# A charge for overlap and a margin against GpSimd in a kernel recorder's count

## The chip, the cores and the metric

The program runs on one core of one Trainium2 chip. The metric is the device time of one execution in microseconds (us). TensorE is PE in the profile (its weight loads are PEld), VectorE is DVE, ScalarE is ACT, GpSimd is POOL and SyncE is SP.

## What is computed

The reference is one inference step of a two-layer decoder trunk in float32. A prompt of 16 learned meta tokens and 1024 tokens and a group of 8 samples of 4 tokens share the weights; the model width is 1024. Cut to what matters:

```python
for l in range(2):
    proj = x @ w_in[l]                      # 4 mixers of 256 columns each, with gates
    a = gated_delta_net(conv(proj.a))       # 4 heads, 64x64 state, chunks of 64
    b = hgrn2(proj.b); c = gla(proj.c)      # gated linear recurrences
    d = retention(rope(proj.d))             # fixed decay
    m = concat(norm(a), norm(b), norm(c), norm(d)) * silu(gates) @ w_out[l]
    x = layer_norm(ALPHA * x + m)
    x = layer_norm(ALPHA * x + (silu(x @ w_gate[l]) * (x @ w_up[l])) @ w_down[l])
```

It returns the outputs of both groups, the last rows of the convolution and the states of all heads.

## The kernel before

All tokens stand as 1072 columns in three groups of 304, 384 and 384 (`GROUPS`). A dense product is made of fp32r products: weights and activations are split into a high and a low part (`splits`, `split_out`, `ffn_split`), and each product is three matmuls on line 833. The high part is a copy on ACT (L855), the low part a subtraction, which may run on DVE (L864) or on POOL (L866). A layer has three stretches: the input projection with the four mixers working beside it, the output projection with a layer norm, and the feed-forward part (FFN) with its layer norm. The small products of the mixers fill the same PE queue as the dense ones.

The order of all instructions is found when the program is built, by a recorder (`Kern.run`). Each part of the work is a thread: `main` for the dense products, four mixer workers, the weight loads and splits, the layer norms, and small helpers. A thread gives operations (`Op`), each with an engine, a cost in nanoseconds and what it reads and writes. The recorder keeps a clock for each engine (`clk`) and the time at which each range of memory is ready (`t_data`). Over and over it takes, among the operations whose predecessors are recorded, the one with the earliest start, and `emit` records it, advances its engine's clock by the cost, and marks its output ready a latency later (`LATENCY`). Every engine then runs its own instructions in the recorded order, with semaphores between the engines. So the costs in this count never stand on the chip; they only decide the order, and the engine where there is a choice.

A choice is offered by `tt2`: a `tensor_tensor` with no operand in PSUM is given as a pair, one for DVE and one for POOL, and the recorder takes the one that ends first in its count. The costs before are `68 + 1.042 * n` for DVE and `147 + 2.1 * n` for POOL, with n the elements in a partition. Some operations have no choice. On POOL always: the zeroing memsets (`zero`, L927), two products in each `delta_unit`, and the gain and shift of the residual in `residual` (512 wide) and `save_x` (256 wide), in which `tt` is called with "POOL". On DVE always: all that reads PSUM (tile `banks`), and `stt` (L877), `ts` (L902, unless the pair offers ACT), `dcopy` (L907), scans, transposes and the statistics of the norms.

Of the kernel before, what the change touches and what calls it, by code (L numbers as in the profile page):

```python
# [213 lines left out]
class V:  # L214
# [4 lines left out]
    def __init__(self, ap, sp, lo, hi, part=0):  # L219
        self.ap, self.sp, self.lo, self.hi, self.part = ap, sp, lo, hi, part  # L220
# [54 lines left out]
class P(V):  # L275
# [41 lines left out]
    def range(self):  # L317
        return range(self.h.at + self.lo, self.h.at + self.hi)
# [14 lines left out]
    return tuple(range(row // 32, (row + a) // 32)), tuple(range(col // 32, (col + b) // 32)), (a, b)  # L333


LATENCY = {"PE": 196.0, "DVE": 128.0, "ACT": 131.0, "POOL": 76.0}


class Wait:
# [95 lines left out]
class Kern:  # L435
    def __init__(self, tc, ins, outs):
        self.tc, self.nc, self.i, self.o = tc, tc.nc, ins, outs
        self.clk = {e: 0.0 for e in ("PE", "ACT", "DVE", "POOL", "SP", "DMA", "HW")}
        self.mode, self.pe_end = (128, 128), 0.0
        self.t_load = [0.0] * 4  # L440
        self.t_start, self.t_end = {}, [[0.0] * 4 for _ in range(4)]
        self.switches = 0
        self.tick, self.cols, self.warm = 0, 0.0, False
        self.duty, self.duty_t = 0.0, 0.0
        self.nc.scalar.preload_act_table_set(TABLES[AF.Exp])
        self.w_t = np.zeros(NCOL // 16 + 2)
        self.r_t = np.zeros(NCOL // 16 + 2)
        self.pw_t = [0.0] * 8
        self.pr_t = [0.0] * 8
        self.dw_t = {}  # L450
        self.table = TABLES[AF.Exp]
        self.clk["ACT"] = 1283.0
        self.threads = []
        self.flags = {}
        self.cur = None
# [185 lines left out]
    def emit(self, op, t0):  # L641
        e = op.eng
        cost = op.cost
        if e == "ACT" and op.table and op.table != self.table:
            self.nc.scalar.preload_act_table_set(op.table)  # L645
            self.table = op.table
            t0 += 1283
        op.fn()
        if e == "SP":
            self.clk["SP"] = t0 + 60  # L650
            q = max(t0 + 600, self.clk["HW"])
            self.clk["HW"] = q + 480
            d0 = max(q + 900, self.clk["DMA"])
            self.clk["DMA"] = d0 + cost
            end = rend = d0 + cost + 500
        else:
            if e == "PE":
                rq, cq, mode = op.tile
                k = int(t0 / TICK)
                if k > self.tick:  # L660
                    self.warm = k == self.tick + 1 and self.cols >= FULL
                    self.tick, self.cols = k, 0.0
                self.cols += op.work
                slow = 1 if self.warm else 2
                td = self.t_data(op)
                if mode != self.mode:
                    td = max(td, self.pe_end + DRAIN)
                    self.mode = mode
                    self.switches += 1
                for _ in range(op.passes):  # L670
                    a = max(td, self.t_start.get((rq, cq), 0.0), *(self.t_load[r] for r in rq)) + WLOAD * op.cols * slow
                    b = max(a, *(self.t_end[r][c] for r in rq for c in cq))
                    f = b + op.cost * slow
                    for r in rq:
                        self.t_load[r] = a
                        for c in cq:
                            self.t_end[r][c] = f
                    self.t_start[rq, cq] = b
                t0 = max(t0, b) if len(rq) + len(cq) < 8 else t0
                cost = f - t0 if len(rq) + len(cq) == 8 else 6.0  # L680
                self.pe_end = max(self.pe_end, f)
                self.duty = self.duty * math.exp((self.duty_t - t0 - cost) / SPAN) + op.work / 2.4 / SPAN
                self.duty_t = t0 + cost
            self.clk[e] = t0 + cost
            end = rend = (f if e == "PE" else t0 + cost) + LATENCY[e]
        for v in op.rd:
            if v.sp == "s":
                a, b = v.lo // 16, (v.hi + 15) // 16
                np.maximum(self.r_t[a:b], rend, out=self.r_t[a:b])
            elif v.sp == "p":  # L690
                for k in v.range():
                    self.pr_t[k] = max(self.pr_t[k], rend)
        for v in op.wr:
            if v.sp == "s":
                a, b = v.lo // 16, (v.hi + 15) // 16
                np.maximum(self.w_t[a:b], end, out=self.w_t[a:b])
            elif v.sp == "p":
                for k in v.range():
                    self.pw_t[k] = max(self.pw_t[k], end)
            else:  # L700
                self.dw_t[v.lo] = max(self.dw_t.get(v.lo, 0.0), end)
# [47 lines left out]
    def run(self):  # L749
        self.cur = None  # L750
        while True:
# [9 lines left out]
            for th in self.threads:  # L761
                open_bank = False
                for pos, e in enumerate(th.q):
                    if not e.ops:
                        continue
                    new = any(h.at is None for h in e.banks)
                    skip = e.deps or new and open_bank
                    open_bank |= new
                    if skip:
                        continue  # L770
                    tb = 0.0
                    if new:
                        hs = [h for h in e.banks if h.at is None]
                        ks = self.places(hs)
                        if ks is None:
                            continue
                        tb = max(self.bank_time(k, h.n) for k, h in zip(ks, hs))
                    if e.td is None:
                        e.td = [max(self.t_data(o) for o in e.run)] if len(e.run) > 1 else [self.t_data(o) for o in e.ops]
                    pick = None  # L780
                    for op, td in zip(e.ops, e.td):
                        t = max(td, tb, self.clk[op.eng])
                        x = t
                        if op.eng == "ACT" and op.table and op.table != self.table:
                            x += 1283
                        if pick is None or x + op.cost < pick[0] + pick[1].cost:
                            pick = (x, op)
                    if pick[1].eng == "PE":
                        tiled = pick[1].tile[2] != FULLM
                        if tiled and self.mode == FULLM:  # L790
                            pick = (max(pick[0], max(e.td[0], tb) + HOLD), pick[1])
                        elif not tiled and self.mode != FULLM:
                            pick = (max(pick[0], self.clk["PE"] + SLACK), pick[1])
                    k = (pick[0], URGENT if pick[1].eng != "PE" and any(h.main for h in e.banks) else th.prio, pos)
                    if th.name == "main" and pick[1].eng == "PE" and self.duty < KEEP and pick[0] <= self.clk["PE"]:
                        k = (self.clk["PE"] - 1.0, th.prio, pos)
                    if best is None or k < best[0]:
                        best = (k, pick[1], th, e)
# [3 lines left out]
            _, op, th, e = best  # L802
# [58 lines left out]
    def tt(self, out, a, b, op, eng="DVE"):  # L861
        if eng == "DVE":
            return Op("DVE", 68 + 1.042 * out.n,
                      lambda: self.nc.vector.tensor_tensor(out=out.x(), in0=a.x(), in1=b.x(), op=op), (a, b), (out,))  # L864
        return Op("POOL", 147 + 2.1 * out.n,
                  lambda: self.nc.gpsimd.tensor_tensor(out=out.x(), in0=a.x(), in1=b.x(), op=op), (a, b), (out,), 27.0)  # L866

    def stt(self, out, a, s, b, op0, op1):
# [1784 lines left out]
```

## Time and profile before

| | us |
|---|---|
| median of 3 runs | 3169.23 (3167.81 to 3171.99) |
| profiled execution, its own time | 3172.53 |
| span of that execution | 3170.8 |
| PE busy | 3018.0 |
| DVE busy | 1731.3 |
| ACT busy | 1111.1 |
| POOL busy | 529.6 |

The span runs from the first to the last instruction; the execution's own time is 1.7 us longer. The mean granted clock of TensorE is 0.977 of full speed. The chain that ended last is the way back from the last instruction to whatever released it, step by step; here it reaches back to 554 us. Matmuls are pipelined and their ends are modelled, so that a busy PE can still be waiting for operands between matmuls.

### The profile page before, as it was taken

How to read it: one execution, taken by the hardware profiler on the slowest of the kernel's cores; microseconds unless marked ns; L12 is line 12 of the kernel's file. 1: busy time of each engine (PE TensorE's matmuls, PEld its weight loads, DVE VectorE, ACT ScalarE, POOL GpSimd, SP SyncE). 2: the span in 40 equal slices, each digit the busy share in tenths (PEclk: the TensorE clock that was granted, in tenths of full speed). 3: DMA queues.
4: the chain of work that ended last, by engine and by line, in shares of the span. 5: the costliest groups of instructions: out<-in, count | busy, mean ns of one | idle time of the engine just before them, and what ended most of it. 6: DMA issues, size and time to landing. Idle time of an engine off the chain costs nothing.

```text
span 3170.8 us, 65772 instructions
## 1 busy us (share of the span) xinstructions
PE 3018.0 (95%) x27758; PEld 2733.2 (86%) x27758; DVE 1731.3 (55%) x3978; ACT 1111.1 (35%) x2310; POOL 529.6 (17%) x617
## 2 busy tenths in 40 slices
PE   7999999989999999999999989999999999999996
PEld 5778887878899999999977778879789999999996
DVE  8886668556633333333497856783774333333336
ACT  5454577432411111111264437763433111111113
POOL 3412213010600000000044211230115000000001
PEclk8999999999999999999999999999999999999998
DMA  5310221241111111111033102123511111111112
GB/s 199 110 49 27 66 64 61 90 158 57 60 54 47 47 40 41 53 47 47 34 125 92 48 26 69 62 65 96 177 47 63 41 40 54 47 47 47 47 40 75
DMA packets 121030, 210.94 MB, mean 67 GB/s; under 512 B 32336, under 2 KB 81488, under 8 KB 120608
## 3 DMA queue, kind: packets, MB, share of 16 engines
q1 hardware_dynamic: 120736, 206.75, 19.7%
q8 instruction: 217, 3.56, 0.5%
q14 instruction: 77, 0.63, 0.1%
HBM read 162.28 MB, written 40.04 MB: 64 GB/s over the span
## 4 chain that ended last, share of the span: by engine, by line
PE 65%; DVE 9%; ACT 3%; DMA 2%; issue 2%; POOL 1%; SPq 0%; DVEq 0%; ACTq 0%; POOLq 0%
PE banks L833 63%; DVE H L864 2%; DVE R L864 2%; DVE H L877 1%; PE banks L839 1%; DVE P L864 1%; ACT H L858 1%; DVE H L902 1%; DVE H L1012 1%; ACT R L855 1%; ACT P L858 1%; ACT L645 0%; DMA H<-XR 0%; DMA H<-OF 0%; POOL H L866 0%
## 5 line engine op out<-in xcount | busy, mean ns | idle before, releaser
L833 PE MATMUL banks<-R 128*128 128x384 f32 (+3 forms) x11840 | 2106.8, 334 | 36.7 <-DVE R L864 13.8
L833 PEld LDWEIGHTS banks<-R 128*128 128x128 f32 x11840 | 1939.0, 191 | 103.9 <-DVE R L864 23.1
L864 DVE TENSOR_TENSOR H<-H,banks 128x512 f32<-128x512 f32 (+6 forms) x722 | 407.3, 568 | 534.6 <-PE banks L833 531.8
L864 DVE TENSOR_TENSOR R<-H,R 128x1024 fp32r<-128x1024 f32 (+5 forms) x356 | 347.8, 987 | 444.6 <-ACT R L855 442.2
L855 ACT CAST R<-H 128x1024 fp32r<-128x1024 f32 (+3 forms) x358 | 284.7, 811 | 803.8 <-PE banks L833 712.0
L833 PE MATMUL banks<-R,P 128*128 128x512 f32 x1584 | 371.7, 394 | 0.0
L833 PEld LDWEIGHTS banks<-R,P 128*128 128x128 f32 x1584 | 296.2, 188 | 66.8 <-issue 0.6
L866 POOL TENSOR_TENSOR H<-H 128x256 f32<-128x256 f32 (+10 forms) x267 | 237.3, 903 | 331.0 <-ACT H L858 81.8
L866 POOL TENSOR_TENSOR P<-H,P 128x384 fp32r<-128x384 f32 (+7 forms) x49 | 73.6, 1503 | 1303.6 <-ACT P L855 1283.4
L858 ACT ACTIVATE H<-H 128x384 f32<-128x384 f32 (+11 forms) x455 | 189.7, 434 | 191.0 <-DVE H L1014 78.9
L833 PE MATMUL banks<-H 32*32 32x32 f32 (+15 forms) x6134 | 203.7, 224 | 22.2 <-issue 8.3
L833 PEld LDWEIGHTS banks<-H 32*32 32x32 f32 (+9 forms) x6134 | 146.8, 121 | 79.5 <-issue 42.8
L833 PE MATMUL banks<-P 32*32 32x32 f32 (+10 forms) x5982 | 170.7, 215 | 26.5 <-DVE P L864 12.4
L833 PEld LDWEIGHTS banks<-P 32*32 32x32 f32 (+6 forms) x5982 | 124.2, 118 | 75.7 <-issue 36.9
L855 ACT COPY H<-banks 128x384 f32<-128x384 f32 (+14 forms) x305 | 112.0, 374 | 219.9 <-PE banks L833 176.6
L855 ACT CAST P<-H 128x304 fp32r<-128x304 f32 (+2 forms) x132 | 64.3, 487 | 284.8 <-DVE H L864 284.8
L864 DVE TENSOR_TENSOR H<-H 128x384 f32<-128x384 f32 (+12 forms) x310 | 131.8, 442 | 50.5 <-ACT H L858 28.9
L858 ACT ACTIVATE H<-banks 128x384 f32<-128x384 f32 (+5 forms) x169 | 72.0, 429 | 228.9 <-PE banks L833 223.5
L839 PE MATMUL banks<-H 128*128 128x128 f32 (+3 forms) x639 | 114.0, 302 | 36.1 <-DVE H L902 16.2
L833 PE MATMUL banks<-P,R 128*128 128x304 f32 (+1 forms) x1056 | 147.4, 299 | 0.0
L833 PEld LDWEIGHTS banks<-P,R 128*128 128x128 f32 x1056 | 145.9, 188 | 0.0
L839 PEld LDWEIGHTS banks<-H 128*128 128x128 f32 (+3 forms) x639 | 77.9, 148 | 69.6 <-DVE H L902 19.0
(86 smaller groups left out, 1714.6 us busy)
## 6 DMA issues: line engine op xcount, KB each, us to landing
H<-in_wst SPq DMA_DIRECT2D x208, 512.0 KB, 3.2
XR<-H SPq DMA_DIRECT2D x12, 512.0 KB, 4.2
GF<-H SPq DMA_DIRECT2D x32, 192.0 KB, 2.2
H<-XR SPq DMA_DIRECT2D x4, 1536.0 KB, 6.7
H<-OF SPq DMA_DIRECT2D x28, 192.0 KB, 4.0
H<-XR SPq DMA_DIRECT2D x41, 128.0 KB, 3.0
XR<-H SPq DMA_DIRECT2D x41, 128.0 KB, 1.8
H<-in_xin SPq DMA_DIRECT2D x8, 512.0 KB, 7.6
```

The source lines that it names most:

```text
L833: return Op("PE", cost, lambda: self.nc.tensor.matmul(out=out.x(), lhsT=lhsT.ap, rhs=rhs.ap, start=start, stop=stop), (lhsT, rhs), (out,), ...
L839: return Op("PE", 0.83 * p + 2.5, lambda: self.nc.tensor.transpose(out=out.x(), in_=in_.ap, identity=i.ap), (in_,), (out,), 20, None, tile ...
L855: fn = lambda: self.nc.scalar.copy(out=out.x(), in_=in_.x())
L858: fn = lambda: self.nc.scalar.activation(out=out.x(), in_=in_.x(), func=f, scale=s, bias=b)
L864: lambda: self.nc.vector.tensor_tensor(out=out.x(), in0=a.x(), in1=b.x(), op=op), (a, b), (out,))
L866: lambda: self.nc.gpsimd.tensor_tensor(out=out.x(), in0=a.x(), in1=b.x(), op=op), (a, b), (out,), 27.0)
L877: lambda: self.nc.vector.scalar_tensor_tensor(out=out.x(), in0=a.x(), scalar=sc, in1=b.x(), op0=op0, op1=op1),
L902: return Op("DVE", 68 + ptr + rate * out.n, lambda: self.nc.vector.tensor_scalar(out=out.x(), in0=a.x(), **kw), rd, (out,))
L1012: yield Op("DVE", 68 + 1.05 * 512, lambda o=o, s=s: nc.vector.bn_stats(out=o, in_=s.x()), (s,), (st,))
```

## The change

Three things are changed, all in the recorder's count. The latencies after DVE, ACT and POOL are larger (128 to 138, 131 to 158, 76 to 92 ns). A DVE operation that reads no PSUM is charged the time by which it overlaps the last recorded POOL operation, up to `SHARED` = 300 ns; `pool_t` is that operation's start. In the choice between DVE and POOL, POOL has 300 ns added, and POOL's cost of a `tensor_tensor` is `147 + 2.7 * n`.

```diff
-LATENCY = {"PE": 196.0, "DVE": 128.0, "ACT": 131.0, "POOL": 76.0}
+LATENCY = {"PE": 196.0, "DVE": 138.0, "ACT": 158.0, "POOL": 92.0}
+SHARED = 300.0
...
+        self.pool_t = 0.0
...
     def emit(self, op, t0):
         e = op.eng
         cost = op.cost
+        if e == "DVE" and not any(v.sp == "p" for v in op.rd):
+            cost += min(SHARED, max(0.0, min(t0 + cost, self.clk["POOL"]) - max(t0, self.pool_t)))
+        elif e == "POOL":
+            self.pool_t = t0
...
-                        if pick is None or x + op.cost < pick[0] + pick[1].cost:
+                        if pick is None or x + op.cost + (SHARED if op.eng == "POOL" else 0) < pick[0] + pick[1].cost:
...
-        return Op("POOL", 147 + 2.1 * out.n,
+        return Op("POOL", 147 + 2.7 * out.n,
```

## Rows read from the trace of the kernel before

**Rows 1.** The page's busy times: us, share of the span, instructions.

```profile
PE 3018.0 (95%) x27758; PEld 2733.2 (86%) x27758; DVE 1731.3 (55%) x3978; ACT 1111.1 (35%) x2310; POOL 529.6 (17%) x617
```

**Rows 2.** Windows by stretch: length, busy us of PE, PEld, DVE, ACT, POOL, granted clock.

```profile
0.00:554.00 554.00, 500.91 (x7674) 423.54 (x7674) 411.83 (x1225) 310.69 (x727) 151.29 (x225) 0.95 0.26 82
554.00:840.00 286.00, 264.96 (x1812) 230.36 (x1813) 182.03 (x347) 110.55 (x225) 50.18 (x42) 0.95 0.30 95
840.00:1571.00 731.00, 731.00 (x4258) 699.90 (x4258) 255.58 (x379) 124.74 (x192) 57.78 (x39) 1.00 0.13 46
1571.00:2390.00 819.00, 764.22 (x9567) 657.39 (x9566) 582.91 (x1565) 419.80 (x940) 196.65 (x260) 0.97 0.25 80
2390.00:3120.00 730.00, 730.00 (x4314) 698.84 (x4313) 256.65 (x387) 126.20 (x197) 62.38 (x44) 1.00 0.14 48
3120.00:3171.00 51.00, 26.87 (x140) 23.20 (x138) 42.31 (x77) 19.12 (x32) 11.32 (x8) 0.80 0.23 85
```

**Rows 3.** The page's chain that ended last, shares of the span by engine.

```profile
PE 65%; DVE 9%; ACT 3%; DMA 2%; issue 2%; POOL 1%; SPq 0%; DVEq 0%; ACTq 0%; POOLq 0%
```

**Rows 4.** Two pieces of that chain, in order: start, length, what.

```profile
811.19 2.96 POOL R L866
...
821.06 2.22 DVE R L864
```

**Rows 5.** Waits of PE: releaser, us in total, times, longest us.

```profile
PE banks L839 <- DVE H L902: 16.2, 8, 4.3
PE banks L833 <- DVE P L864: 14.8, 19, 2.0
...
PE banks L833 <- DVE R L864: 13.8, 18, 2.4
...
PE banks L833 <- POOL P L866: 5.6, 6, 1.9
```

**Rows 6.** Groups of POOL's instructions by form, whole span: count, busy us, mean ns.

```profile
L866 POOL TENSOR_TENSOR H<-H 128x512 f32<-128x512 f32 x59 | 82.0, 1420 | 49.3 <-ACT H L858 40.3 <-DMA H<-in_lnb 8.7
L866 POOL TENSOR_TENSOR H<-H 128x256 f32<-128x256 f32 x92 | 71.4, 782 | 69.7 <-DMA H<-XR 33.5 <-PE banks L833 18.7 <-DVE H L914 7.0
L866 POOL TENSOR_TENSOR P<-H,P 128x384 fp32r<-128x384 f32 x38 | 66.3, 1745 | 1251.4 <-ACT P L855 1251.4
```

**Rows 7.** POOL's memsets, all forms together, whole span.

```profile
L927 POOL MEMSET P<- 128x512 f32 (+8 forms) x52 | 22.6, 440 | 196.1 <-DVE P L864 64.3 <-PE banks L833 46.4 <-DVE P L918 31.1
L927 POOL MEMSET H<- 128x768 f32 (+7 forms) x36 | 18.3, 508 | 113.8 <-DVE H L918 65.4 <-PE banks L833 36.2 <-DMA out_hs<-H 4.6
```

**Rows 8.** Groups of DVE's instructions by form, whole span.

```profile
L864 DVE TENSOR_TENSOR R<-H,R 128x1024 fp32r<-128x1024 f32 x208 | 261.8, 1259 | 436.1 <-ACT R L855 435.3 <-ACT P L858 0.7
L864 DVE TENSOR_TENSOR H<-H,banks 128x512 f32<-128x512 f32 x315 | 215.3, 684 | 176.3 <-PE banks L833 176.1
L864 DVE TENSOR_TENSOR R<-H,R 128x384 fp32r<-128x384 f32 x101 | 64.5, 662 | 5.9 <-ACT R L855 5.1
...
L864 DVE TENSOR_TENSOR P<-H,P 128x384 fp32r<-128x384 f32 x50 | 30.5, 610 | 26.7 <-ACT P L855 26.7
```

**Rows 9.** The same view of DVE within the first FFN, 900 to 1500 us.

```profile
L864 DVE TENSOR_TENSOR H<-H,banks 128x512 f32<-128x512 f32 x96 | 66.0, 688 | 68.9 <-PE banks L833 68.9
L864 DVE TENSOR_TENSOR R<-H,R 128x1024 fp32r<-128x1024 f32 x51 | 62.4, 1223 | 172.9 <-ACT R L855 172.9
...
L864 DVE TENSOR_TENSOR P<-H,P 128x384 fp32r<-128x384 f32 x17 | 9.5, 558 | 9.9 <-ACT P L855 9.9
```

**Rows 10.** Timeline of DVE, 820 to 840 us: start, length, instruction.

```profile
820.99 2.30 DVE L864 TENSOR_TENSOR R<-H,R 128x1024 fp32r<-128x1024 f32 x1
```

**Rows 11.** Timeline of POOL, 820 to 840 us.

```profile
819.23 12.05 POOL L866 TENSOR_TENSOR H<-H 128x512 f32<-128x512 f32 x8
```

**Rows 12.** The page's costliest group of DVE, reading PSUM.

```profile
L864 DVE TENSOR_TENSOR H<-H,banks 128x512 f32<-128x512 f32 (+6 forms) x722 | 407.3, 568 | 534.6 <-PE banks L833 531.8
```

**Rows 13.** Timeline of POOL, 2300 to 2480 us.

```profile
2414.46 7.15 POOL L866 TENSOR_TENSOR H<-R 128x288 f32<-128x288 f32 x8
```

## The prediction

> **What bounds the kernel now.** I begin with the busy times of the page [rows 1]: PE works 3018 of 3171 us, DVE 55% of the span, POOL 17%. That average mixes two kinds of stretches, so the windows come next [rows 2]. In both FFN stretches (731 and 730 us) PE is busy the whole time at the full granted clock, with DVE at 35%. Nothing that DVE or POOL does there can be worth much. All that can move lies in the other 1710 us: 840 us of the first layer's mixers, output projection and layer norm, 819 us of the second's, and 51 us at the end. There PE is idle 53 + 21 + 55 + 24 = 153 us, the granted clock is 0.95 to 0.97, and DVE is busy 412 + 182 + 583 + 42 = 1219 us, or 71%.
>
> The chain that ended last [rows 3] says what sets the end: PE 65%, DVE 9% (285 us), POOL 1% (between 16 and 48 us by rounding; I take 25). It reaches back to 554 us. Behind that point and outside the FFNs DVE is busy 182 + 583 + 42 = 807 us and POOL 50 + 197 + 11 = 258 us [rows 2]. So 285 / 807 = 0.35 of DVE's work and 25 / 258 = 0.10 of POOL's lies on the path. I use both shares for all 1710 us. Two pieces show what such a place looks like [rows 4]: at 811 us the path goes through a POOL operation for 2.96 us, at 821 us through a DVE operation for 2.22 us. The waits of PE are the third view [rows 5]: those ended by DVE are 16.2, 14.8 and 13.8 us in the largest of the rows shown, the largest by POOL 5.6 us.
>
> **The change, part by part.** No instruction is added. Those that have a choice may move from POOL to DVE, and the recorded order changes.
>
> *How many have the choice.* POOL has 617 instructions [rows 1]. 88 are memsets of 40.9 us together [rows 7], four more set constants. 525 `tensor_tensor` of about 488 us remain. By the code 168 of them must stay: 48 in `residual` at 1420 ns (68 us), 96 in `save_x` at 782 ns (75 us) [rows 6], and 24 in `delta_unit`, for which I take 1 us each (24 us). So 357 operations of 321 us could move, 0.90 us each.
>
> *How many move.* Before, POOL is taken where DVE could start later than POOL by more than 79 + 1.058n ns; now it is 379 + 1.658n. For n = 384 that is 485 before and 1016 now, for 128 it is 214 and 591, for 1024 it is 1162 and 2077. All 208 weight splits of width 1024 stand on DVE [rows 8], and no group of POOL of that width exists: in those 208 choices DVE was never 1162 ns later. A lag is mostly the rest of one DVE operation, so a limit of 1016 will rarely be passed. Against that, at 2414 us eight operations of 288 columns in a row stand on POOL [rows 13], which needs a lag of several us; the margin of 300 would not turn these. I take 70%, with bounds of 40 and 95%: 250 operations, 225 us. POOL's busy time falls to about 300 us.
>
> *Where they come from.* In the FFN stretches POOL does 120 us [rows 2]; some 27 of the `residual` operations fall there (about 36 us), so 84 us of the 321 can move without any effect, because PE is full. Outside, 237 us remain, of which 70% are 166 us or 184 operations.
>
> *What DVE pays.* An undisturbed 384-wide operation takes 558 ns on DVE [rows 9]; the movable ones are narrower on average, and I take 0.45 us. 184 x 0.45 = 83 us more on DVE.
>
> *What DVE gets back.* The 1024-wide split takes 1223 ns in the FFN and 1259 over the span, the 384-wide subtraction 558 against 662 (into R) and 610 (into P), while a 512-wide operation that reads PSUM takes 688 and 684 [rows 8, 9]. So what reads SBUF alone is lengthened where POOL works, and what reads PSUM is not: the new charge is laid on the right operations. The three lengthened groups lose 7.5 + 10.5 + 2.6 = 20.6 us of 357 us, 6%; the worst of them 16%. Of DVE's 1731 us at least 407 read PSUM [rows 12]; I take 1000 us as reading SBUF alone and estimate the loss at 80 us, with bounds of 58 and 160. POOL operations that must stay are 167 of 488 us. Two thirds of the loss can go, and 70% of that does: 37 us.
>
> At one place the whole size can be seen: the split at 820.99 takes 2.30 us, 1.08 more than undisturbed, beside a row of POOL operations of 1.5 us each [rows 10, 11]. The Trainium skill (SBUF — State Buffer, "SBUF: two separate sides") says that VectorE with two SBUF inputs and GpSimd take turns on a shared pair of ports, which whoever starts first holds for its whole instruction. This row agrees. By that rule a cap of 300 ns is too small a charge; what it would make of the time is rival 2.
>
> *On the path.* DVE gains 83 - 37 = 46 us of work; at 0.35 that is +16 us. POOL loses 166 us; at 0.10 that is -17 us. The direct exchange is nothing, -1 us.
>
> *The tail.* After 3120 us the path is DVE's, which is busy 42 of 51 us, and POOL has 8 operations [rows 2], all with the choice and 512 wide. Moved, they cost DVE 8 x 0.69 = 5.5 us at the undisturbed time of that width [rows 9], and at the 37 / 184 = 0.2 us of relief each, 1.6 us come back: +4 us.
>
> *The order.* Longer latencies, the charge and the dearer POOL cost nothing themselves; they place whatever waits for DVE and POOL later in PE's queue and dense products in front of it. Where the old count was too short, PE stood still in its fixed order. The waits of PE ended by DVE or POOL are 50 us in the four rows shown [rows 5] and some 90 in all 25 rows of that view. Bounds: nothing (other operations are late in their place), and 90. A 384-wide POOL operation shows how short the old count was: counted as 953 ns, 1745 measured in the FFN splits [rows 6]. I take a fifth of 90, -19 us, because most of these waits follow layer norms, where no other work is at hand.
>
> *Sum.* -1 + 4 - 19 = -16 us from the profiled 3172.5, whose own time is 3.3 us above the median: 3156.5 there, **3153 us** against the median of 3169.2. I call anything within 0.2% (6 us) the same, about what this kernel's runs can tell.
>
> **The rivals.**
> 1. *DVE becomes the queue (slower).* DVE is 71% busy outside the FFNs. If moved operations delay the path by that share and not by 0.35, and the order gains nothing, it is 83 x 0.71 - 37 x 0.35 - 17 + 4 = +33 us: 3202. For it: at the end the path is DVE's throughout. Against it: 0.35 is what the chain shows. With the order's -19 kept, the share must pass 0.54 for a loss. Chance 0.24, lighter forms included.
> 2. *The two engines block each other for whole instructions (much faster).* Then a moved POOL operation of 0.90 us frees DVE wherever it would have worked on SBUF alone: 0.71 x 1000 / 1731 = 0.41 of the time, 0.37 us each, 68 us and not 37. DVE gains 15 us of work, 5 on the path: 3142, and with twice the gain in order 3123. The Trainium skill's rule (SBUF — State Buffer, "SBUF: two separate sides") is this at full size. For it the split at 821 us, against it the mean loss of 6%. Chance 0.14.
> 3. *Nothing.* POOL is 1% of the chain; its operations are hidden and stay hidden on DVE, and PE's waits only move: 3163 to 3175. Chance 0.11.
> 4. *The change does not do what it says.* DVE's count runs several us ahead of POOL's as at 2414 us, under a third moves, and the order is merely shuffled: about 3166. Chance 0.06.
>
> **How the numbers follow.** The forecast has 0.45 with a range of its own of 3131 to 3164. With rival 2 the faster side has 0.57 (a little of both falls within 0.2%); same is 0.18; slower 0.25. The range reaches to most of rivals 1 and 2: 3112 to 3200.
>
> **What would show each step.** POOL busy near 300 us with 230 to 300 fewer `tensor_tensor`, 512- and 256-wide groups left at full count; DVE near 1800 us (250 x 0.45 more, 37 less); the 384-wide subtraction into R near 580 ns; both FFN stretches within 3 us of 731 and 730; PE's idle time outside them down by 15 to 20 us; POOL on the chain below 1%. It would be wrong if the new order, not the engines, decides: at 0.95, about a tenth of the time outside the FFNs is granted 1.2 GHz in place of 2.4, and a changed mixture of small and dense products can add to it or take from it. It would also be wrong if DVE's waits on PE's path grow in the layer norms, where every step is DVE's.

## The result, and the profile after

The changed kernel takes 3125.12 us (median of four runs, 3118.43 to 3128.17) against 3170.61 us: 0.9854 of the time before, 95% interval 0.9835 to 0.9873, or 45 us less. Timed again later beside other runs of before it gave 0.9854 (0.9835 to 0.9872). The forecast was 3153 us, a gain of 16 us; the direction was right and the gain nearly three times as large.

The profiled execution took 3118.43 us with a span of 3116.3 us. Lines of the changed kernel from the middle on stand six further down: DVE's `tensor_tensor` is L870, POOL's L872. In the rows H, P and R are the program's buffers in SBUF, and `banks` is PSUM. The page's busy times, beside [rows 1]:

```profile
PE 2987.8 (96%) x27758; PEld 2712.0 (87%) x27758; DVE 1750.8 (56%) x4142; ACT 1111.4 (36%) x2313; POOL 391.2 (13%) x444
```

POOL has lost 173 instructions and 138 us, DVE has 164 more and only 20 us. PE's idle time is 3116.3 - 2987.8 = 128.5 us, 24 less than before, and its busy time is 30 us shorter with the same number of matmuls. The mean granted clock is 0.986 in this profile and was 0.977 in that of before; how much of the 30 us goes with it is taken up further down. The windows by stretch, cut where the FFNs now begin and end, beside [rows 2]:

```profile
0.00:554.00 554.00, 504.75 (x7848) 427.38 (x7849) 423.32 (x1316) 315.97 (x738) 113.28 (x169) 0.97 0.26 83
554.00:798.00 244.00, 236.57 (x1603) 206.92 (x1602) 162.68 (x324) 104.52 (x206) 25.33 (x19) 0.99 0.35 110
798.00:1535.00 737.00, 737.00 (x4295) 705.87 (x4294) 268.82 (x394) 127.04 (x197) 53.03 (x36) 1.00 0.14 46
1535.00:2339.00 804.00, 756.24 (x9596) 653.39 (x9595) 587.28 (x1632) 418.22 (x943) 146.58 (x185) 0.98 0.26 81
2339.00:3066.00 727.00, 727.00 (x4290) 695.76 (x4290) 266.31 (x395) 126.55 (x198) 51.69 (x36) 1.00 0.14 47
3066.00:3117.00 51.00, 26.22 (x136) 22.64 (x134) 42.37 (x84) 19.12 (x32) 1.29 (x1) 0.79 0.23 85
```

The FFNs take 737 + 727 us in place of 731 + 730, with the small differences in what of the neighbouring work falls within them: 4295 matmuls after 4258 in the first, 4290 after 4314 in the second, and the time for each is the same within 0.2%. The whole difference lies in the two mixer stretches: 798 us in place of 840, and 804 in place of 819. In the first, 42 us shorter, PE is idle 56.7 us in place of 74.1 and busy 741 in place of 766, at a higher granted clock (0.97 and 0.99 after 0.95 and 0.95). At the end DVE is as busy as before, though POOL has one operation there and not eight.

PE's largest waits after, beside [rows 5] (releaser, us in total, times, longest us):

```profile
PE banks L839 <- DVE P L870: 19.3, 22, 3.0
...
PE banks L845 <- DVE H L908: 7.0, 4, 2.6
...
PE banks L839 <- DVE R L870: 3.1, 7, 0.8
```

The wait on the layer norm's scaling (L902, now L908) has gone from 16.2 to 7.0 us, that on the split's low part in R from 13.8 to 3.1. The one on DVE's `tensor_tensor` results in P has grown from 14.8 to 19.3. Over all rows of the view the waits ended by DVE or POOL add up to 73.7 us after 95.6. The groups of POOL by form, beside [rows 6]:

```profile
L872 POOL TENSOR_TENSOR H<-H 128x256 f32<-128x256 f32 x93 | 74.5, 812 | 97.6 <-DMA H<-XR 52.4 <-ACT H L864 12.6 <-DVE H L883 12.3
L872 POOL TENSOR_TENSOR H<-H 128x512 f32<-128x512 f32 x50 | 72.2, 1479 | 73.9 <-ACT H L864 64.2 <-DMA H<-in_lnb 9.7
L872 POOL TENSOR_TENSOR P<-H,P 128x384 fp32r<-128x384 f32 x20 | 39.0, 1949 | 1271.7 <-ACT P L861 1271.7
```

What has no choice stays (the first form, and 48 of the second), the third form has gone from 38 to 20, and each of the three takes longer on average than before (812, 1479 and 1949 ns after 782, 1420 and 1745). DVE's groups, beside [rows 8]:

```profile
L870 DVE TENSOR_TENSOR R<-H,R 128x1024 fp32r<-128x1024 f32 x208 | 259.2, 1246 | 436.1 <-ACT R L861 435.3 <-ACT P L861 0.5
L870 DVE TENSOR_TENSOR H<-H,banks 128x512 f32<-128x512 f32 x313 | 214.2, 685 | 180.5 <-PE banks L839 180.5
L870 DVE TENSOR_TENSOR R<-H,R 128x384 fp32r<-128x384 f32 x108 | 75.7, 728 | 3.8 <-ACT R L861 2.7
...
L870 DVE TENSOR_TENSOR P<-H,P 128x384 fp32r<-128x384 f32 x68 | 40.7, 598 | 26.2 <-ACT P L861 26.2
```

The 1024-wide split is 13 ns shorter on average, the 384-wide subtraction into R 66 ns longer. So the collisions have not simply gone where POOL's work has. By engine, the chain that ended last beside [rows 3]; it reaches back to 670 us here and to 554 us before:

```profile
PE 66%; DVE 7%; ACT 2%; DMA 2%; issue 1%; POOL 1%; SPq 0%; DVEq 0%; ACTq 0%; POOLq 0%
```

### The profile page after: what moved, and what is told of

Same layout as the page of the kernel before. It is cut to its first block, busy times and chain, and to the rows that moved or that the text cites. A ratio compares the mean times of both kernels' runs of the same rounds, so it can differ in the third digit from the quotient of the medians.

```text
span 3116.3 us, 65676 instructions
## 1 busy us (share of the span) xinstructions
PE 2987.8 (96%) x27758; PEld 2712.0 (87%) x27758; DVE 1750.8 (56%) x4142; ACT 1111.4 (36%) x2313; POOL 391.2 (13%) x444
## 4 chain that ended last, share of the span: by engine, by line
PE 66%; DVE 7%; ACT 2%; DMA 2%; issue 1%; POOL 1%; SPq 0%; DVEq 0%; ACTq 0%; POOLq 0%
PE banks L839 64%; DVE H L870 2%; PE banks L845 1%; DVE P L870 1%; DVE H L883 1%; DVE R L870 1%; ACT H L864 1%; ACT R L861 1%; DMA H<-OF 0%; DVE H L1018 0%; POOL R L872 0%; DVE H L908 0%; DMA P<-H 0%; ACT P L864 0%; DVE P L913 0%
## 5 line engine op out<-in xcount | busy, mean ns | idle before, releaser
L870 DVE TENSOR_TENSOR H<-H,banks 128x512 f32<-128x512 f32 (+5 forms) x708 | 401.1, 570 | 522.3 <-PE banks L839 518.0
L870 DVE TENSOR_TENSOR R<-H,R 128x1024 fp32r<-128x1024 f32 (+5 forms) x376 | 358.9, 967 | 444.7 <-ACT R L861 442.0
L861 ACT CAST R<-H 128x1024 fp32r<-128x1024 f32 (+4 forms) x361 | 285.9, 806 | 817.7 <-PE banks L839 720.8
L864 ACT ACTIVATE H<-H 128x384 f32<-128x384 f32 (+12 forms) x477 | 204.5, 445 | 206.2 <-DVE H L1020 86.0
L872 POOL TENSOR_TENSOR H<-H 128x256 f32<-128x256 f32 (+8 forms) x206 | 194.6, 962 | 290.6 <-ACT H L864 116.1
L839 PE MATMUL banks<-H 32*32 32x32 f32 (+11 forms) x5884 | 187.2, 224 | 18.8 <-DVE H L870 6.3
L872 POOL TENSOR_TENSOR P<-H,P 128x384 fp32r<-128x384 f32 (+1 forms) x22 | 39.5, 1798 | 1274.0 <-ACT P L861 1271.7
L839 PEld LDWEIGHTS banks<-H 32*32 32x32 f32 (+6 forms) x5884 | 133.3, 120 | 75.2 <-issue 39.3
L839 PE MATMUL banks<-P 32*32 32x32 f32 (+14 forms) x6240 | 181.1, 214 | 15.7 <-DVE P L870 9.8
L839 PEld LDWEIGHTS banks<-P 32*32 32x32 f32 (+10 forms) x6240 | 132.0, 117 | 63.4 <-issue 27.5
L861 ACT COPY H<-banks 128x384 f32<-128x384 f32 (+14 forms) x313 | 115.8, 376 | 181.2 <-PE banks L839 143.3
L870 DVE TENSOR_TENSOR H<-H 128x384 f32<-128x384 f32 (+14 forms) x389 | 155.3, 417 | 43.8 <-ACT H L864 25.7
L845 PE MATMUL banks<-H 128*128 128x128 f32 (+4 forms) x642 | 109.0, 290 | 30.3 <-DMA H<-in_cst 7.7
```

The source lines that it names most:

```text
L839: return Op("PE", cost, lambda: self.nc.tensor.matmul(out=out.x(), lhsT=lhsT.ap, rhs=rhs.ap, start=start, stop=stop), (lhsT, rhs), (out,), ...
L845: return Op("PE", 0.83 * p + 2.5, lambda: self.nc.tensor.transpose(out=out.x(), in_=in_.ap, identity=i.ap), (in_,), (out,), 20, None, tile ...
L861: fn = lambda: self.nc.scalar.copy(out=out.x(), in_=in_.x())
L864: fn = lambda: self.nc.scalar.activation(out=out.x(), in_=in_.x(), func=f, scale=s, bias=b)
```

## The experiments

Three theories were set against each other. A: the engine counts; work that leaves POOL stops blocking DVE and leaves the path. B: the order counts; longer counts move PE's waiting work back in its fixed queue. C: any new order moves the time by a per cent or so, and the gain is luck. A ratio is always against runs of before taken beside it on the same chip.

### The three parts, each alone

**pick_only**: the margin and POOL's cost of 2.7, without the charge and with the old latencies.

> Only the choice is changed: margin of 300 and POOL's dearer cost; no charge for overlap, old latencies. Theory A (the engine counts: work that leaves POOL stops blocking DVE): most of the gain, 0.986 to 0.991 of before, POOL busy near 390 us. Theory B (the order counts: longer counts place PE's waiting work later): the choice alone gives little, 0.995 to 1.003. Theory C (any shuffle of the order moves the time by about one per cent): anywhere from 0.985 to 1.01, without relation to POOL's busy time.

Measured: 3138.86 us, 0.9931 (0.9913 to 0.9948), POOL busy 390.7 us. As much work leaves POOL as in the whole change, and about half of the gain comes. This lies between what A (0.986 to 0.991) and B (0.995 to 1.003) expected and decides nothing between them.

**charge_only**: the charge in `emit`, nothing else.

> Only the charge of up to 300 ns for a VectorE operation beside a GpSimd one; old choice, old cost of GpSimd, old latencies. Theory A: little, 0.996 to 1.004, since GpSimd keeps its work (busy 520 us or more, as a charged VectorE loses more choices). Theory B: 0.988 to 0.994, PE's idle time down by 15 us or more. Theory C: 0.985 to 1.01.

Measured: 3124.95 us, 0.9892 (0.9865 to 0.9919). Its page's busy times:

```profile
PE 2990.0 (96%) x27758; PEld 2714.6 (87%) x27758; DVE 1732.1 (55%) x3939; ACT 1113.6 (36%) x2318; POOL 556.8 (18%) x646
```

POOL does more than before, 557 us after 530, because a charged DVE loses more choices, and about three quarters of the gain of the whole change come (1.1 of 1.5%). That speaks against A.

**lat_only**: the three latencies, nothing else.

> Only the three latencies. Theory A: 0.997 to 1.003. Theory B: 0.990 to 0.997, PE's idle time down by some 10 us. Theory C: 0.985 to 1.01.

Measured: 3142.55 us, 0.9937 (0.9916 to 0.9959), PE's idle time 142.5 us. The three parts alone give 0.7, 1.1 and 0.6%, together 1.5%: they do not add.

### How much a mere shuffle does

Each control changes one latency by 1 ns, which breaks ties otherwise.

```diff
# shuffle_a, shuffle_b, shuffle_c: before with one of
-LATENCY = {"PE": 196.0, "DVE": 128.0, "ACT": 131.0, "POOL": 76.0}
+LATENCY = {..., "DVE": 129.0, ...}
+LATENCY = {..., "ACT": 132.0, ...}
+LATENCY = {..., "POOL": 77.0}
# after_shuffle: the changed kernel with
+LATENCY = {"PE": 196.0, "DVE": 139.0, "ACT": 158.0, "POOL": 92.0}
```

> A control: VectorE's latency counted as 129 in place of 128 ns, which means nothing for the chip but breaks ties otherwise and so shuffles the order. Theories A and B: 0.997 to 1.003. Theory C: a move of 0.5% or more either way.

> A second control: ScalarE's latency counted as 132 in place of 131 ns. The first control gave 0.9968. Theories A and B: 0.996 to 1.002. Theory C (chance of the order): a scatter as wide as the effects of the parts, so 0.988 or 1.008 would be no surprise.

> A third control: GpSimd's latency counted as 77 in place of 76 ns. Theories A and B: 0.996 to 1.002. Theory C: as in the second control. Whatever the time, TensorE's busy time should follow the time granted at 1.2 GHz, by about half a us for each us, as in the six profiles so far.

> A control around the changed kernel: VectorE's latency counted as 139 in place of 138 ns. Three controls around the kernel before gave 0.9968, 0.9955 and 0.9992. If the change's gain is its own, this stays within 0.4% of the changed kernel: 0.982 to 0.990 of before. If it is luck of one order: 0.990 or more.

Measured: 0.9968 (0.9956 to 0.9980), 0.9955 (0.9941 to 0.9970) and 0.9992 (0.9975 to 1.0009) around before, and 0.9864 (0.9846 to 0.9882) around the changed kernel. The first two lie just outside what A and B expected. So chance of the order is worth a few tenths of a per cent, and all three controls fall on the same side, the third within its noise: the order of before may have been a poor draw. Against the mean of before and its three controls, 0.9979, the change is worth 0.9854 / 0.9979 = 0.9875. C explains some 0.2 of the 1.5%, not the rest. The expectation that TensorE's busy time follows the time at 1.2 GHz held for shuffle_c in direction (3008 us after 3004 and 3002 in the two other controls, at a granted clock of 0.981 after 0.984 and 0.985), at about a quarter of a us for each us and not half. It did not hold everywhere: flat_100 and after_flat_100, below, have 2996 and 2992 us at 0.980 and 0.974.

### The engine and the order apart

**no_pick**: the changed kernel with the old choice and the old cost of POOL, so the charge and the latencies.

> The change without its choice part: charge and latencies, but the old choice and GpSimd's old cost, so GpSimd keeps some 550 us of work. Theory A (the engine counts): slower than the whole change by 0.5% or more, 0.991 to 0.996. Theory B (the order counts): as good as the whole change, 0.983 to 0.989. Theory C: 0.985 to 1.005.

Measured: 3120.66 us, 0.9864 (0.9831 to 0.9896), POOL busy 550.2 us. The part of the change that moves work from POOL to DVE can be left out.

**before_on_dve** and **after_on_pool** keep the recorded order of one kernel and exchange the engine of those operations on which the two choices differ.

```diff
# before_on_dve (266 operations); after_on_pool likewise, with the old
# choice asked and p.fn put in place of d.fn (201 operations)
             run = e.run if len(e.run) > 1 else [op]
+            if len(e.ops) == 2 and op.eng == "POOL":
+                d, p = e.ops
+                x, y = (max(self.t_data(o), self.clk[o.eng]) for o in e.ops)
+                if not y + p.cost + 0.6 * p.wr[0].n + 300.0 < x + d.cost:
+                    op.fn = d.fn
             for o in run:
```

> The order and the count of before, but 266 operations that it counts as GpSimd's, and that the new choice would not give to it, are issued on VectorE at the same place in the order. GpSimd keeps some 260 tensor_tensor. Theory A (the engine counts): 0.986 to 0.993. Theory B (the order counts): 0.997 to 1.005, since PE's order is that of before.

> The order and the count of the changed kernel, but the 201 operations that its choice gives to VectorE and the old choice would give to GpSimd are issued on GpSimd at the same place. Theory A: the gain goes, 0.994 to 1.002 of before. Theory B: most of it stays, 0.984 to 0.991.

Measured: 3163.35 us, 0.9993 (0.9977 to 1.0010), and 3123.94 us, 0.9859 (0.9844 to 0.9874). The instructions of PE and ACT stand in the same order as in before and in the changed kernel. The pages' busy times of the first,

```profile
PE 2999.9 (95%) x27758; PEld 2714.9 (86%) x27758; DVE 1759.8 (56%) x4244; ACT 1111.9 (35%) x2310; POOL 293.5 (9%) x351
```

and of the second:

```profile
PE 2990.4 (96%) x27758; PEld 2714.6 (87%) x27758; DVE 1727.8 (55%) x3941; ACT 1110.9 (36%) x2313; POOL 542.3 (17%) x645
```

With POOL's work nearly halved and before's order there is no gain; with before's load on POOL and the new order there is all of it. This refutes A: in this kernel it does not matter, within about 0.2% either way, which of the two engines does these operations. The waits of PE in before_on_dve,

```profile
PE banks L838 <- DVE R L869: 15.8, 25, 3.1
...
PE banks L844 <- DVE H L907: 13.9, 9, 2.6
```

are those of before: 13.8 and 16.2 us in [rows 5], and 3.1 and 7.0 in the changed kernel.

### Does the charge have to be right?

**flat_charge** and **flat_100** add the same number to every DVE operation that reads no PSUM, blind to POOL; 25 ns is the mean of the charge.

```diff
         cost = op.cost
+        if e == "DVE" and not any(v.sp == "p" for v in op.rd):
+            cost += 25.0        # flat_100: 100.0
```

> Before, with 25 ns added in the count to every VectorE operation that reads no PSUM: the same sum as the charge for overlap (53 us over 2137 operations in the recorder's count), spread evenly and blind to GpSimd. If the charge works because it knows where the two engines collide (theory B, exact): 0.996 to 1.001. If any longer count does it (theory B, plain caution): 0.987 to 0.992, as the charge alone gave 0.989. If it is chance of the order (theory C): 0.985 to 1.005.

> The flat charge four times as large: 100 ns for every VectorE operation that reads no PSUM. If plain caution works by placing PE's waiting work later: as good as or better than 25 ns (0.9919), 0.984 to 0.992, with less idle time of PE than 135 us. If the counts merely have to be right: worse than with 25 ns, 0.993 to 1.002.

Measured: 0.9919 (0.9891 to 0.9947), and 3125.92 us, 0.9864 (0.9848 to 0.9881). A blind 100 ns does all that the change does, with PE's idle time at 128.6 us and still more work on POOL:

```profile
PE 2995.7 (96%) x27758; PEld 2726.3 (87%) x27758; DVE 1719.8 (55%) x3864; ACT 1132.8 (36%) x2356; POOL 590.1 (19%) x693
```

So the charge works as caution, and need not know where the engines collide. Whether the same sum does a little more where they collide (charge_only, 0.9892) than spread evenly (flat_charge, 0.9919) is within the noise. The two waits followed above part here, that on the layer norm's scaling first, that on the split's low part in R second (lines stand two further down than in before):

```profile
PE banks L841 <- DVE H L904: 16.7, 4, 8.0
...
PE banks L835 <- DVE R L866: 4.2, 12, 0.6
```

The second is short, as in the changed kernel; the first is as long as before, though the time is that of the changed kernel. It has no such tie to the gain.

### Whose order?

**pe_later_120** and **pe_later_320** are before with the distance that the count keeps between operands and a TensorE operation set to 120 and 320 ns in place of 20; no cost of DVE or POOL is touched. **after_pe_120** and **after_pe_220** are the changed kernel with 120 and 220.

```diff
 # mm, and tr likewise: the argument behind the outputs
-                  (lhsT, rhs), (out,), 20, None, tile_of(...)
+                  (lhsT, rhs), (out,), 320, None, tile_of(...)
```

> Before, with one number changed: every TensorE operation is counted as able to start 120 ns behind its operands in place of 20. If TensorE's waiting work placed later carries the gain: 0.984 to 0.992, idle time of PE under 140 us, its waits ended by VectorE under 70 us. If it is VectorE's own order that counts: 0.996 to 1.003.

> The same with 320 ns. If TensorE's place in the order carries the gain and caution is cheap: 0.980 to 0.990; the mixers' chains become longer in the count by some 0.3 us at each product, so at some size it must turn: 0.990 to 1.0 if that is already here. If VectorE's own order counts: 0.996 to 1.01.

> The changed kernel with the 120 ns for TensorE. If the change's counts are still too short for TensorE: 0.976 to 0.983 of before, faster than the changed kernel (0.985). If the change already has all of it: 0.983 to 0.990.

Measured: 0.9921 (0.9900 to 0.9941), 0.9884 (0.9864 to 0.9905), and 0.9831 (0.9812 to 0.9851) for the changed kernel with 120. With 320 ns the waits of PE in the same two places as above are 9.2 and 7.7 us:

```profile
PE banks L833 <- DVE R L864: 9.2, 15, 1.6
PE banks L839 <- DVE H L902: 7.7, 6, 2.3
```

With 120 ns PE's idle time (145.2 us) and its waits ended by DVE (71.8 us) missed the 140 and 70 that were expected, and with 320 ns the time lies where 0.980 to 0.990 was expected. Counting PE's operations later, with no cost of another engine touched, gives 1.2% of the 1.5. This is B, and points to PE's order. It does not isolate it: whatever follows a product is counted later too, so DVE's order and some choices of engine change as well (POOL has 585 instructions after 617).

**after_flat_100**: the changed kernel with 100 ns more on every DVE operation that reads no PSUM.

> The changed kernel with 100 ns more on every VectorE operation that reads no PSUM. Two sorts of caution that each gave 0.985 to 0.986 of before: if they do the same thing, 0.982 to 0.989; if they add, 0.970 to 0.980.

Measured: 3135.91 us, 0.9899 (0.9884 to 0.9914). The two cautions do not add; together they are slower than each alone. PE's idle time is 142.9 us again, at a granted clock of 0.974 in that profile.

To see whether 120 ns on the changed kernel is a gain, it was put beside the changed kernel itself, with a larger step.

> The changed kernel once more, beside the next one: 0.984 to 0.987 of before by every theory.

> The changed kernel with TensorE counted 220 ns behind its operands in place of 20. If its counts are still too short for TensorE: 0.978 to 0.983, faster than the changed kernel beside it. If it already has all that caution gives: 0.984 to 0.990, as with 100 ns more on VectorE (0.9899), which lost part of the gain.

Measured: 0.9854 (0.9835 to 0.9872) and 0.9853 (0.9829 to 0.9877). As far as these intervals tell, the changed kernel has all that this caution gives. The fastest median seen, 3112.29 us with 120 ns, cannot be told from the changed kernel's by these intervals.

One rival to caution was left untested: no run made a count shorter. That more caution helps, and not simply any other order than that of before, rests on the controls by 1 ns and on the larger gain of the larger step (25 to 100 ns, 120 to 320 ns).

## Why the prediction was right or wrong, step by step

- *How many move.* 70% were taken; 525 `tensor_tensor` on POOL became 352, so 173 of the 357, 48%, within the bounds of 40 to 95. POOL's busy time is 391 us and not 300. The argument from the 1024-wide splits (a lag is mostly the rest of one operation) was too strong, and the row of eight operations that spoke against it was right: the additions of the form H<-R are still on POOL, 31 after 29.
- *What DVE pays and gets back.* 164 more operations at the 0.45 us of the prediction are 74 us; DVE is 20 us busier, so by this estimate 54 us came back where 37 outside the FFNs were forecast. Yet the 384-wide subtraction into R went from 662 to 728 ns, not to 580.
- *On the path: -1 us.* The net is right, and shown by exchange: before_on_dve is at 0.9993, -2 us with an interval of -7 to +3. Whether its two terms of 16 and 17 us are, no run shows. The shares of the chain behind them are weak: in before_on_dve the chain reaches back to 1 us, DVE has 16% of it, and the time is that of before.
- *The tail: +4 us.* It is 51 us in both, with DVE busy 42.3 and 42.4 us: no loss. DVE's 512-wide operations there, before and after, show why:

```profile
L864 DVE TENSOR_TENSOR H<-H 128x512 f32<-128x512 f32 x24 | 18.7, 804 | 0.1
L870 DVE TENSOR_TENSOR H<-H 128x512 f32<-128x512 f32 x31 | 20.2, 678 | 0.1
```

  Seven more cost 1.5 us, because each takes 678 ns in place of 804; six one-column `stt` beside them give back 1.2 us (351 to 144 ns each). The lengthening went almost whole, where the sum let 1.6 of 5.5 us come back.
- *The FFNs.* Right to within the cut of the windows: 1464 us for 1461. (The 27 operations of POOL put there at about 36 us are 38 by the 1.42 us of the rows; nothing hangs on it.)
- *The order: -19 us.* **This is the step that failed, in size.** The mechanism that it names is the one that the runs show, but it carries the whole gain: 45 us by after_on_pool (0.0141 x 3166), not 19. It was sized as a fifth of PE's waits that end on DVE or POOL ("some 90"; the rows add up to 95.6). Those waits fell by about that much; what they left out is the rest. The profiles of before_on_dve and of the changed kernel show it at nearly the same granted clock (0.985 and 0.986), the one in the order of before, the other in the new: the span falls from 3156.1 to 3116.3 us, by 40. Of these PE's idle time takes 28 (156.2 to 128.5): 18 in waits ended by DVE or POOL (92.1 to 73.7), 9 in waits put down to others (of them "issue", for which the profile shows no releaser, 14.5 to 2.8). The other 12 lie where PE counts as busy (2999.9 to 2987.8). The sum had no term for either of these two.
- *The rivals.* The time lies at the edge of rival 2 (3123 to 3142), but not for its reason. The Trainium skill (SBUF — State Buffer, "SBUF: two separate sides") has the loser of the shared ports blocked for the whole instruction; single rows before agreed. What follows for the time here is nothing, because exchanging 266 operations between the engines moved it by less than 0.3% either way. Rival 1, DVE as the queue, did not come: DVE rose by 20 us and the kernel became faster. (Its part of the chain fell from 9 to 7%, but the two chains reach back differently far.) The prediction's own sign of being wrong, that the new order and not the engines decides, is what came; its clock part is small, as follows.

Why PE's busy time is shorter is settled in part only. Of the 30 us between the profiles of before and after, 18 are there between two profiles with PE's order of before, 3018.0 us at a granted clock of 0.977 (before) and 2999.9 at 0.985 (before_on_dve, whose engines alone were exchanged, at no gain): they go with the clock, or with the run, and not with the order. The profile of before was one of its low-clocked runs, which makes the two profiles look further apart than the medians are. Over the 64 runs of before beside these experiments, the time went from 3155 to 3177 us and the mean granted clock from 0.985 to 0.977 with it. A granted clock can be turned into time at the lower of its two levels, 1.2 GHz (half speed for twice the missing share); against that the time rises by 0.30 us for each us (correlation 0.76). In the four runs of the changed kernel the granted clock was 0.982 to 0.986. The mean time at 1.2 GHz falls by 14 us, from 115.8 to 101.5, which by that slope is an estimated 4 us of the 45. The 12 us that remain may be waits too short to stand out between pipelined matmuls; no run tested that.

## What to carry to other kernels

In this kernel an order is planned by costs and every engine then runs its queue in that order. Here counts that were too short cost more than counts made somewhat longer: the engine that is the bottleneck stood still behind late operands. Too much caution lost again (0.9899 with two sorts together, after 0.985 to 0.986 with either). Test such a change by keeping the order and exchanging only the engine, and the engine with the order exchanged; a gain from a "more accurate" cost can be plain caution, as the blind 100 ns shows. And time a few orders that differ by a nanosecond before a per cent is put down to a reason.

## What the runs showed of the hardware that was not expected

Moving 266 operations from POOL to DVE took 236 us off POOL and added only 29 us to DVE (529.6 to 293.5, 1731.3 to 1759.8 us), less than 0.11 us each, although a 384-wide one takes 0.56 us on DVE when undisturbed: at the 0.45 us of the prediction the 266 would have cost 120 us, so by this estimate some 90 us came back as lengthening that went. It did not go everywhere. The 384-wide subtraction into R went from 662 to 612 ns and that into P from 610 to 593, but the 208 splits of width 1024 take 1260 ns on average after 1259, though POOL's busy time nearly halved: the work that moved is not what makes them longer than the 1223 ns of the FFN. Two engines that collide like this can trade work at little charge in busy time, and still not move the end.
